# The v projection's causal convolution with tokens on the partitions: shifted rows by DMA in place of transposes, and a later opening of the late tiles

## The chip, the cores and the metric

The kernel runs on one core of one Trainium2 chip. The metric is device time in microseconds (us) of one execution. Before the change the median of three runs is 1875.9 us (1875.82 to 1875.97).

## The reference

One decoder layer over 256 tokens of width 2048, all in float32. Cut to what bears on the change:

```python
xn = rms_norm(h, ln_mix_g)                      # (256, 2048)
proj = einsum('btd,de->bte', xn, w_in)          # q, k, v, z, b, a, sc_b, sc_c, sc_h, gate_a, gate_b
qkv = silu(causal_dwconv(concat([q, k, v]), conv_w))   # 4 taps along the tokens, per channel
#   causal_dwconv: y[t] = sum_i x[t - 3 + i] * w[i]
q, k = l2_norm(q), l2_norm(k)                   # per head of 128 channels
o_a = gated_delta_chunked(q, k, v, g, beta)     # 16 heads; then rms_norm(o) * silu(z)
o_b = sc_b * causal_dwconv(sc_c * sc_h, conv_sc_w)
merged = sigmoid(gate_a) * (o_a @ w_proj_a) + sigmoid(gate_b) * (o_b @ w_proj_b)
h = h + merged @ w_out
ff = silu(hn @ w_gate) * (hn @ w_up);  out = rms_norm(h + ff @ w_down)
```

## The kernel before

**Tiling.** The 256 tokens are two halves (m = 0, 1) of 128. Every projection is cut into pieces of 512 output columns, called products: `product` (from L392) multiplies all 16 (for the last matrix 44) blocks of 128 input rows with one such piece. A matrix product is done three times, high part by high part, low by high and high by low, because float32 operands are split into two parts that TensorE takes. The weights come in groups of two blocks: `raw` (128 rows by 1024 numbers, 512 KB, by DMA from L263 in `fetch`), then `wh` by ScalarE (ACT), the rounded high part, then `wl` by VectorE (DVE), the rest. `ensure` issues them four groups ahead of TensorE. There are four `raw` buffers and four each of `wh` and `wl`. `raw36` is the load of group 36; a product with 16 blocks takes eight groups, so groups 0 to 7 are the first k product, 8 to 15 the first q product, and so on.

**Two forms of a product.** With `chan=True` the channels lie on the partitions of the result: 24 matmuls of 256 columns a group, 192 a product. With `chan=False` the tokens do: 12 matmuls of 512 columns a group, 96 a product.

**The order of the products.** For each of four groups g of four heads: k, z of the group before (from g = 1 on), q, v. Then for n = 0 to 3 the three short convolution products scc, sch and scb (with z of the last group after the first scc). Then gates, projections, w_out, and the feed-forward part.

**What sets the order of the rest.** All instructions are issued by hand in an order that a Python planner writes: `Pace` holds estimated times of each engine, every piece of work beside the products is a generator (`post_qk`, `post_v`, `core`, `post_b`, ...) that yields a due time, and `step` puts its next instructions between the matmuls when the planner thinks that they are due. Each engine runs its instructions in the order written, and so does SP's DMA queue: a DMA that has to wait holds up all DMAs behind it. The tickets in `turn` let the generators pass one after the other.

**v before.** In `post_v` (L800) the first v product (g = 0) has its channels on the partitions and is evacuated by DVE; the other three have tokens there, are evacuated by ACT (`rows_v`) and turned by DVE in 16 pieces (`flip`, `fc_v`). The convolution then runs along the free axis with four ACT and twelve DVE instructions (`conv`, `cv_v`), ACT applies silu, TensorE turns the result back with eight transposes a group (`vt`), and ACT scales and evacuates it in eight pieces to `v`. `core` uses `v` in `solve`.

**The late tiles.** `post_b` (L1164) ends an scb product. For n = 1 it first waits until the last head group is finished (`oc`), since `open_late` frees that group's memory and opens new tiles there; only then does it evacuate its PSUM tile. `product` allows one product with an unevacuated result when the next begins.

Of the kernel before, what the change touches and what calls it, by code (L numbers as in the profile page):

```python
# [9 lines left out]
F32 = mybir.dt.float32  # L10
F32R = mybir.dt.float32r
I32 = mybir.dt.int32
AF = mybir.ActivationFunctionType
ALU = mybir.AluOpType

P = 128
T = 256
D = 2048
KD = D // P
H = 16  # L20
HG = 4
NG = H // HG
DFF = 5632
KF = DFF // P
W = 512
# [7 lines left out]
MM = 4  # L33
LOWLAG = 1
EARLY = 16
LAG = 500.0
LOAD = 271
SOON = -1
# [161 lines left out]
def tile_gdn_shortconv_layer(  # L200
# [13 lines left out]
    ln_ffn: bass.AP,  # L214
    ln_fin: bass.AP,
    cqkv: bass.AP,
    csc: bass.AP,
    a_log: bass.AP,
    dt_bias: bass.AP,
# [4 lines left out]
    pace = Pace()  # L224
    pe = Lane(pace, nc.tensor, "pe")
    act = Lane(pace, nc.scalar, "act")
    dve = Lane(pace, nc.vector, "dve")
    pool = Lane(pace, nc.gpsimd, "pool")
    PS = bass.MemoryType.PSUM
    NS = D // W  # L230
# [15 lines left out]
    apool = pool_of("apool", 1)  # L246
    const = pool_of("const", 1, top=True)
    rawpool = pool_of("rawpool", 2, top=True)
    io = pool_of("io", 2, top=True)
# [6 lines left out]
    gp = pool_of("gp", 1, stack=pg)  # L256

    def bank(nm):
        return ps_sm.tile([P, 512], F32, tag="sm", name=nm)

    def fetch(dst, src, free=0.0):

        nc.sync.dma_start(dst, src)  # L263
        start = max(pace.t["dma"], free)
        pace.t["dma"] = start + 4.0 * math.prod(dst.shape) / 360.0
        pace.note(dst, "dma", True, pace.t["dma"] + Pace.DMA_LAG)

    def both(out, a, b, op):

        dve.scalar_tensor_tensor(out=out, in0=a, scalar=1.0, in1=b, op0=ALU.mult, op1=op)  # L270
# [4 lines left out]
    def pair(pool, tag, nm):  # L275
        t = pool.tile([P, 2, HG, T], F32R, tag=tag, name=nm)
        return t[:, 0], t[:, 1]
# [96 lines left out]
    def need(key, n=0):  # L374
        while key not in st:
            yield n
        if at[key] + LAG > pace.t["pe"]:
            pace.end = max(pace.end, at[key])
            yield n
# [3 lines left out]
    turn = [0, 0]  # L383
# [64 lines left out]
    ident = gp.tile([P, P], F32, name="ident")  # L448
# [15 lines left out]
    sel = gp.tile([P, HG, SQ], F32R, name="sel")  # L464

    g_ffn = const.tile([P, KD], F32, name="g_ffn")
    wc = gp.tile([P, 3 * H, 4], F32, name="wc")
    wsc = const.tile([P, KD, 3], F32, name="wsc")
    alog = gp.tile([P, H], F32, name="alog")
    dtb = gp.tile([P, H], F32, name="dtb")  # L470
# [37 lines left out]
    rx_row = gp.tile([P, T], F32, name="rx_row")  # L508

    def evac_chan(pt, dst, b):  # L510

        if len(b.shape) == 2:
            b = b.unsqueeze(1).broadcast_to([P, HG, T])
        for m in range(2):
            cs = slice(2 * m, 2 * m + 2)
            dve.tensor_tensor(
                dst[:, cs], pt[m].rearrange("p (c t) -> p c t", t=T), b[:, cs], op=ALU.mult
            )
        close(pt)

    def bc(ap, n):
        return ap.unsqueeze(2).broadcast_to([P, ap.shape[1], n])

    def rows_tile(nm):
        return io.tile([P, 2, W], F32, tag="rows", name=nm)

    def full_tile(nm):
        return io.tile([P, HG, T], F32, tag="rows", name=nm)

    def chan_tile(nm):  # L530
        return io.tile([P, HG, T], F32, tag="cv", name=nm)
# [3 lines left out]
    def evac_rows(pt, dst, func=AF.Copy):  # L535
        for m in range(2):
            act.activation(dst[:, m, :], pt[m], func, scale=rx[:, m:m + 1])
        close(pt)

    def flip(rows, ch, when=SOON):  # L540
        src = rows.rearrange("p m (c n) -> p m c n", n=P)
        dst = ch.rearrange("p c (m t) -> p m c t", t=P)
        for i in range(0, P, SQ):
            for j in range(0, P, SQ):
                dve.transpose(
                    out=dst[j:j + SQ, :, :, i:i + SQ], in_=src[i:i + SQ, :, :, j:j + SQ]
                )
            yield when

    def conv(chan, wt, taps, y, when, then=None):  # L550
        for c in range(HG):
            act.activation(y[:, c, :], chan[:, c, :], AF.Copy, scale=wt(c, taps - 1))
        yield
        for c in (0, 2):
            for s in range(1, taps):
                for j in (c, c + 1):
                    dve.scalar_tensor_tensor(
                        out=y[:, j, s:], in0=chan[:, j, :T - s], scalar=wt(j, taps - 1 - s),
                        in1=y[:, j, s:], op0=ALU.mult, op1=ALU.add,
                    )  # L560
            yield when
            if then is not None:
                act.activation(then[:, c:c + 2], y[:, c:c + 2, :], AF.Silu)

    xg = [pair(apool, f"a{n}", f"xg{n}") for n in range(NS)]
    oa = [pair(apool, f"s{n}", f"oa{n}") for n in range(NS)]

# [228 lines left out]
        mark(("sc", g), (s_, vs, rq))  # L798

    def post_v(g, pt, me):  # L800
        while turn[0] < me - 1:
            yield
        nm = f"v{g}"
        if g == 0:
            yield from need("rx_row")
            full = full_tile(f"full_{nm}")
            evac_chan(pt, full, rx_row)
            yield
        else:
            rows = rows_tile(f"rows_{nm}")  # L810
            evac_rows(pt, rows)
            yield
            while turn[0] < me:
                yield
            full = io.tile([P, HG, T], F32, tag="fc", name=f"fc_{nm}", bufs=1)
            yield from flip(rows, full)
        while turn[0] < me:
            yield
        y = chan_tile(f"cv_{nm}")
        yield from conv(full, lambda c, i: wc[:, 2 * H + HG * g + c, i:i + 1], 4, y, 0, y)  # L820
        turn[0] += 1
        yield
        yield from need(("sc", g))
        if g:
            yield from need(("done", g - 1))
        yield 2
        vs = st["sc", g][1]
        v = gp.tile([P, 2, HG, P], F32, tag="v", name=f"v_{g}")
        for m in range(2):
            b = bank(f"vt_{g}_{m}")  # L830
            for c in range(HG):
                pe.transpose(
                    b[:, c * P:(c + 1) * P], y[:, c, m * P:(m + 1) * P], ident
                )
            for c in range(HG):
                act.activation(
                    v[:, m, c, :], b[:, c * P:(c + 1) * P], AF.Copy, scale=vs[:, m, c:c + 1]
                )
        mark(("v", g), v)

    def post_z(g, pt):
# [47 lines left out]
    def core(g):  # L889
# [6 lines left out]
        s_, vs, rq = st["sc", g]  # L896
# [3 lines left out]
        for cp in range(2):  # L900
            pairs = []
            for c in (2 * cp, 2 * cp + 1):
                b = bank(f"gr0_{g}_{c}")
# [14 lines left out]
            b = bank(f"gr1_{g}_{cp}")  # L918
            bv = b.rearrange("p (c q n) -> p c q n", c=2, q=2)
            for j in range(2):  # L920
                c = 2 * cp + j
# [5 lines left out]
            for j in range(2):  # L927
                c = 2 * cp + j
# [36 lines left out]
        for j in range(SQ - 1):  # L965
            n = j // RS + 1
# [83 lines left out]
        v = st["v", g]  # L1050
# [47 lines left out]
        ro, _ = rsqrt(ssq.rearrange("p m c -> p (m c)"), 2 * HG, f"o{g}", 1.0 / P)  # L1098
# [5 lines left out]
        for hp in range(2):  # L1104
            b = bank(f"oc_{g}_{hp}")
            bv = b.rearrange("p (h t) -> p h t", t=T)
            for j in range(2):
                for m in range(2):
                    pe.transpose(bv[:, j, m * P:(m + 1) * P], ov[:, m, 2 * hp + j, :], ident)
            views.append(bv)  # L1110
        for hp, bv in enumerate(views):
            sl = slice(2 * hp, 2 * hp + 2)
            split(oa[g][0][:, sl, :], oa[g][1][:, sl, :], bv)
# [7 lines left out]
    for g in range(NG):  # L1121
        pt = product(xg, KD, f"k{g}", after=None if g else after_first, chan=True)
        if g == 0:
            scalars()
            spawn(spread())
            spawn(scalars2())
        spawn(post_qk(g, 0, pt, ticket()))
        spawn(decay(g))
        last = spawn(core(g))
        if g:  # L1130
            product_z(g - 1)
        pt = product(xg, KD, f"q{g}", chan=True)
        spawn(post_qk(g, 1, pt, ticket()))
        pt = product(xg, KD, f"v{g}", chan=g == 0)
        spawn(post_v(g, pt, ticket()))


# [26 lines left out]
    def post_b(n, pt, me):  # L1164
        while turn[0] < me - 1:
            yield
        if n == 1:
            yield from need(("oc", NG - 1))
            open_late()
        rows = rows_tile(f"scb{n}")  # L1170
        evac_rows(pt, rows)
        yield
        while turn[0] < me:
            yield
        y = st["y", n]
        ch = io.tile([P, HG, T], F32, tag="fc", name=f"bf{n}", bufs=1)
        yield from flip(rows, ch)
        both(y, y, ch, ALU.mult)
        yield SOON
        if n == 0:  # L1180
            ob[0] = pair(apool, f"s{NS}", "ob0")
        split(*ob[n], y)
        turn[0] += 1
# [3 lines left out]
    def open_late():  # L1187
        pg.close()
        lp = late["pool"] = pool_of("late", 1)
        ob[1:] = [pair(lp, f"s{NS + i}", f"ob{i}") for i in (1, 2, 3)]  # L1190
        late["xh"] = lp.tile([P, 2, D], F32, name="xh")
# [256 lines left out]
```

## Time and profile before

| | before |
|---|---|
| median of 3 runs | 1875.9 us |
| profiled execution | 1876.75 us |
| its span (first to last instruction) | 1875.0 us |
| TensorE (PE) busy | 1861.5 us, 99% |
| VectorE (DVE) busy | 1288.7 us, 69% |
| ScalarE (ACT) busy | 920.7 us, 49% |
| GpSimd (POOL) busy | 198.7 us, 11% |
| DMA engines busy, SP's queue | 54.8% of 16 engines |
| moved | 359.21 MB, 192 GB/s in the mean |
| granted TensorE clock, mean | 0.998 of full |

A busy TensorE only says that matmuls overlap without a gap. Whether it is held up is read from the chain that ended last (which engine the time was on) and from the list of waits (who waited for whom, how long in all).

### The profile page before, as it was taken

How to read it: one execution, taken by the hardware profiler on the slowest of the kernel's cores; microseconds unless marked ns; L12 is line 12 of the kernel's file. 1: busy time of each engine (PE TensorE's matmuls, PEld its weight loads, DVE VectorE, ACT ScalarE, POOL GpSimd, SP SyncE). 2: the span in 40 equal slices, each digit the busy share in tenths (PEclk: the TensorE clock that was granted, in tenths of full speed). 3: DMA queues.
4: the chain of work that ended last, by engine and by line, in shares of the span. 5: the costliest groups of instructions: out<-in, count | busy, mean ns of one | idle time of the engine just before them, and what ended most of it. 6: DMA issues, size and time to landing. Idle time of an engine off the chain costs nothing.

```text
span 1875.0 us, 25127 instructions
## 1 busy us (share of the span) xinstructions
PE 1861.5 (99%) x9444; PEld 1579.2 (84%) x9444; DVE 1288.7 (69%) x1826; ACT 920.7 (49%) x1186; POOL 198.7 (11%) x352
## 2 busy tenths in 40 slices
PE   9999999999999999999999999999999999999998
PEld 9999899988888888888888888888888888888886
DVE  6878788688885977454577789666666666645454
ACT  6755665676545445444444455444444444433443
POOL 0018145172170000000000000000000000000000
PEclk9999999999999999999999999999999999999999
DMA  8546545365464556665555565555555555665553
GB/s 305 189 161 203 186 161 198 133 200 196 144 207 140 195 194 213 208 210 195 186 190 192 188 205 188 204 193 195 195 191 192 194 187 191 202 219 195 193 192 134
DMA packets 101546, 359.21 MB, mean 192 GB/s; under 512 B 12320, under 2 KB 12576, under 8 KB 101168
## 3 DMA queue, kind: packets, MB, share of 16 engines
q1 hardware_dynamic: 98432, 349.69, 54.8%
q0 software_dynamic: 2848, 7.90, 1.5%
q8 instruction: 74, 1.21, 0.3%
q14 instruction: 48, 0.39, 0.1%
q10 hardware_dynamic: 144, 0.01, 0.0%
HBM read 354.38 MB, written 3.18 MB: 191 GB/s over the span
## 4 chain that ended last, share of the span: by engine, by line
PE 96%; DVE 2%; ACT 1%; DMA 1%; issue 1%; DVEq 0%; ACTq 0%
PE mm_dn L173 13%; PE mm_fu L173 13%; PE mm_fg L173 13%; PE mm_proj L173 9%; PE mm_gate L173 9%; PE mm_v L173 5%; PE mm_sch L173 5%; PE mm_scb L173 5%; PE mm_out L173 5%; PE mm_scc L173 4%; PE mm_q L173 4%; PE mm_k L173 4%; PE mm_z L173 4%; PE gr L173 1%; DMA raw<-in_w_in_dram 1%
## 5 line engine op out<-in xcount | busy, mean ns | idle before, releaser
L194 DVE SCALAR_TENSOR_TENSOR wl<-raw,wh 128x1024 fp32r<-128x1024 f32 (+1 forms) x652 | 791.4, 1223 | 481.8 <-ACT wh L194 475.8
L194 ACT CAST wh<-raw 128x1024 fp32r<-128x1024 f32 (+1 forms) x652 | 679.8, 1044 | 880.6 <-PE mm_fu L173 132.4
L173 PE MATMUL mm_dn<-wh,ff 128*128 128x512 f32 x704 | 216.8, 389 | 0.0
L173 PE MATMUL mm_fg<-wh,hg 128*128 128x512 f32 x704 | 216.7, 389 | 0.0
L173 PE MATMUL mm_fu<-wh,hg 128*128 128x512 f32 x704 | 216.7, 389 | 0.0
L173 PE MATMUL mm_gate<-wh,xg 128*128 128x512 f32 x512 | 157.5, 389 | 0.0
L173 PEld LDWEIGHTS mm_dn<-wh,ff 128*128 128x128 f32 x704 | 132.1, 188 | 27.6
L173 PEld LDWEIGHTS mm_fg<-wh,hg 128*128 128x128 f32 x704 | 132.1, 188 | 27.4
L173 PEld LDWEIGHTS mm_fu<-wh,hg 128*128 128x128 f32 x704 | 132.1, 188 | 27.4
L173 PE MATMUL mm_fg<-wl,hg 128*128 128x512 f32 x352 | 136.9, 389 | 0.0
L173 PE MATMUL mm_fu<-wl,hg 128*128 128x512 f32 x352 | 136.9, 389 | 0.0
L173 PE MATMUL mm_dn<-wl,ff 128*128 128x512 f32 x352 | 136.9, 389 | 0.0
L173 PEld LDWEIGHTS mm_gate<-wh,xg 128*128 128x128 f32 x512 | 96.1, 188 | 19.9
L173 PE MATMUL mm_gate<-wl,xg 128*128 128x512 f32 x256 | 99.6, 389 | 0.0
L173 PE MATMUL mm_q<-xg,wh 128*128 128x256 f32 x512 | 93.8, 285 | 0.0
L173 PE MATMUL mm_k<-xg,wh 128*128 128x256 f32 x512 | 93.0, 284 | 0.1
L173 PE MATMUL mm_sch<-wh,xg 128*128 128x512 f32 x256 | 79.9, 393 | 1.5 <-ACT scc L194 1.5
L173 PEld LDWEIGHTS mm_k<-xg,wh 128*128 128x128 f32 x512 | 80.3, 193 | 0.6 <-ACT wh L194 0.5
L173 PEld LDWEIGHTS mm_q<-xg,wh 128*128 128x128 f32 x512 | 79.9, 191 | 0.5
L173 PE MATMUL mm_z<-wh,xg 128*128 128x512 f32 x256 | 80.2, 395 | 0.0
L173 PE MATMUL mm_scc<-wh,xg 128*128 128x512 f32 x256 | 79.8, 393 | 0.0
L173 PE MATMUL mm_scb<-wh,xg 128*128 128x512 f32 x256 | 79.1, 390 | 0.0
(261 smaller groups left out, 2973.1 us busy)
## 6 DMA issues: line engine op xcount, KB each, us to landing
raw<-in_w_in_dram SPq DMA_DIRECT2D x284, 512.0 KB, 4.2
raw<-in_w_gate_dram SPq DMA_DIRECT2D x88, 512.0 KB, 4.1
raw<-in_w_up_dram SPq DMA_DIRECT2D x88, 512.0 KB, 4.0
raw<-in_w_down_dram SPq DMA_DIRECT2D x88, 512.0 KB, 4.3
raw<-in_w_pb_dram SPq DMA_DIRECT2D x32, 512.0 KB, 4.3
raw<-in_w_pa_dram SPq DMA_DIRECT2D x32, 512.0 KB, 4.4
raw<-in_w_out_dram SPq DMA_DIRECT2D x32, 512.0 KB, 4.3
raw<-in_w_in_dram SPq DMA_DIRECT2D x8, 256.0 KB, 5.9
```

Source lines behind the costliest of these rows:

```text
L173: return f(*a, **k)
L194: return f(*a, **k)
```

## The change

v keeps its tokens on the partitions in all four groups. The rows that the causal convolution needs from 1, 2 and 3 tokens earlier are made by DMA: for each shift s one copy of 128 - s partitions of `rows_v` to partitions s and up of a tile `sh`, and one of the last s rows of the first half to the first s rows of the second. The four taps' weights are loaded broadcast over all partitions (`wv`, 128 x 2048). Seven DVE instructions of 128 x 1024 multiply and add, ACT applies silu once, and two DVE instructions scale by `vs` into `v`. No transposes are left in `post_v`. The tile `oa` of the last head group is taken later, since its place holds `wv`. In `post_b` the wait and `open_late` stand after the evacuation, the turning and the product, ahead of the split.

```diff
+FAR = 2500.0
-    oa = [pair(apool, f"s{n}", f"oa{n}") for n in range(NS)]
+    oa = [pair(apool, f"s{n}", f"oa{n}") for n in range(NS - 1)]
...
     def post_v(g, pt, me):
         while turn[0] < me - 1:
             yield
-        nm = f"v{g}"
-        if g == 0:
-            yield from need("rx_row")
-            full = full_tile(f"full_{nm}")
-            evac_chan(pt, full, rx_row)
-            yield
-        else:
-            rows = rows_tile(f"rows_{nm}")
-            evac_rows(pt, rows)
-            yield
-            while turn[0] < me:
-                yield
-            full = io.tile([P, HG, T], F32, tag="fc", name=f"fc_{nm}", bufs=1)
-            yield from flip(rows, full)
+        rows = rows_tile(f"rows_v{g}")
+        evac_rows(pt, rows)
+        wv = apool.tile([P, 4, W], F32, tag=f"s{NS - 1}", name=f"wv_{g}")
+        fetch(wv.rearrange("p i n -> p (i n)"), cv_rows[g].partition_broadcast(P))
+        yield
         while turn[0] < me:
             yield
-        y = chan_tile(f"cv_{nm}")
-        yield from conv(full, lambda c, i: wc[:, 2 * H + HG * g + c, i:i + 1], 4, y, 0, y)
+        shifted = {}
+        for s, tag, k in ((1, "fc", {"bufs": 1}), (2, "rows", {}), (3, "cv", {})):
+            t = shifted[s] = io.tile([P, 2, W], F32, tag=tag, name=f"sh{s}_{g}", **k)
+            dve.memset(t[:s, 0, :], 0.0)
+            fetch(t[s:], rows[:P - s], pace.t["pe"])
+            fetch(t[:s, 1, :], rows[P - s:, 0, :])
+        pace.end = max(pace.end, pace.t["dma"] + FAR)
+        y = io.tile([P, 2, W], F32, tag="cv", name=f"y_v{g}")
+        def tap(s, dst, src):
+            both(dst, src, wv[:, 3 - s, :].unsqueeze(1).broadcast_to([P, 2, W]), ALU.mult)
+        tap(0, y, rows)
+        yield
+        for s, t in shifted.items():
+            tap(s, t, t)
+            both(y, y, t, ALU.add)
+            yield
+        act.activation(y, y, AF.Silu)
         turn[0] += 1
...
         for m in range(2):
-            b = bank(f"vt_{g}_{m}")
-            for c in range(HG):
-                pe.transpose(b[:, c * P:(c + 1) * P], y[:, c, m * P:(m + 1) * P], ident)
-            for c in range(HG):
-                act.activation(v[:, m, c, :], b[:, c * P:(c + 1) * P], AF.Copy, scale=vs[:, m, c:c + 1])
+            both(v[:, m], y[:, m].rearrange("p (c n) -> p c n", n=P), bc(vs[:, m], P), ALU.mult)
...
-        pt = product(xg, KD, f"v{g}", chan=g == 0)
+        pt = product(xg, KD, f"v{g}", chan=False)
...
     def post_b(n, pt, me):
-        if n == 1:
-            yield from need(("oc", NG - 1))
-            open_late()
         rows = rows_tile(f"scb{n}")
...
         both(y, y, ch, ALU.mult)
         yield SOON
+        if n == 1:
+            yield from need(("oc", NG - 1))
+            open_late()
```

SP's queue around group 36, the fifth group of the first z product, before the change (a `raw` is a weight load of 128 rows by 1024 numbers):

```order
L263 DMA raw34_1369<-in_w_in_dram 128x1024
L263 DMA raw35_1400<-in_w_in_dram 128x1024
L263 DMA raw36_1441<-in_w_in_dram 128x1024
L263 DMA raw37_1489<-in_w_in_dram 128x1024
L263 DMA raw38_1507<-in_w_in_dram 128x1024
```

And with the change (`sh1_0`, `sh2_0` and `sh3_0` are the rows of the first v product shifted by 1, 2 and 3 tokens):

```order
L265 DMA raw35_1305<-in_w_in_dram 128x1024
L265 DMA sh1_0_1324<-rows_v0_1052 127x1024
L265 DMA sh1_0_1324<-rows_v0_1052 1x16x32
L265 DMA sh2_0_1328<-rows_v0_1052 126x1024
L265 DMA sh2_0_1328<-rows_v0_1052 2x512
L265 DMA sh3_0_1332<-rows_v0_1052 125x1024
L265 DMA sh3_0_1332<-rows_v0_1052 3x512
L265 DMA raw36_1355<-in_w_in_dram 128x1024
L265 DMA raw37_1397<-in_w_in_dram 128x1024
```

Six DMAs stand between two weight loads. In the other three head groups the same six stand behind `raw60`, `raw95` and `raw130`; a seventh (`wv`) stands earlier, behind `raw27`, `raw59`, `raw91` and `raw123`. The one row of `sh1_0`'s second DMA is issued as 16 pieces of 32 numbers, the 127, 126 and 125 rows are issued as they are.

TensorE inside the first z product before the change (`mm_z` are its two PSUM tiles, `vt` the transposes of v):

```order
L173 MATMUL mm_z_1425<-wh_1490,xg_135 128x512 x2
L173 MATMUL mm_z_1425<-wl_1491,xg_135 128x512
L173 MATMUL vt_0_1615<-ident,cv_v_1419 128x128 x4
L173 MATMUL vt_1_1624<-ident,cv_v_1419 128x128 x4
L173 MATMUL mm_z_1424<-wh_1508,xg_136 128x512 x2
L173 MATMUL mm_z_1424<-wl_1509,xg_136 128x512
```

The same matmuls (blocks of the group that reads `xg_135`, then of the next) with the change:

```order
L174 MATMUL mm_z_1339<-wl_1399,xg_135 128x512
L174 MATMUL mm_z_1338<-wh_1398,xg_135 128x512 x2
L174 MATMUL mm_z_1338<-wl_1399,xg_135 128x512
L174 MATMUL mm_z_1339<-wh_1398,xg_135 128x512 x2
L174 MATMUL mm_z_1339<-wl_1399,xg_135 128x512
L174 MATMUL mm_z_1338<-wh_1416,xg_136 128x512 x2
```

No row with `vt` is left on TensorE, here or in the other three groups; nothing takes its place.

ACT near the end of the last head group before the change (`scc2` and `scb1` are evacuations of two products, `oa3` the result of the head group):

```order
L194 CAST wh186_6523<-raw186_6522 128x1024
L194 CAST wh187_6561<-raw187_6560 128x1024
L194 ACTIVATE scc2_6566<-mm0_scc2_6280,rx_132 128x512
L194 ACTIVATE scc2_6566<-mm1_scc2_6281,rx_132 128x512
L194 CAST oa3_140<-oc_3_0_6577 128x512
L194 CAST oa3_140<-oc_3_1_6582 128x512
L194 CAST wh188_6598<-raw188_6597 128x1024
L194 ACTIVATE scb1_6617<-mm0_scb1_6093,rx_132 128x512
L194 ACTIVATE scb1_6617<-mm1_scb1_6094,rx_132 128x512
```

And with the change, where the evacuation of `scb1` stands eight weight groups earlier:

```order
L195 COPY R_3_5483<-rc_3_5896 32x4x32 x8
L195 CAST wh179_6079<-raw179_6078 128x1024
L195 ACTIVATE scb1_6098<-mm0_scb1_5897,rx_132 128x512
L195 ACTIVATE scb1_6098<-mm1_scb1_5898,rx_132 128x512
L195 CAST wh180_6108<-raw180_6107 128x1024
```

It moved ahead of the head group's last steps; `scc2` keeps its place behind them.

## Rows read from the trace of the kernel before

**Rows 1.** The page: busy time, share of the span, instructions of each engine.
```profile
PE 1861.5 (99%) x9444; PEld 1579.2 (84%) x9444; DVE 1288.7 (69%) x1826; ACT 920.7 (49%) x1186; POOL 198.7 (11%) x352
```

**Rows 2.** The page: the chain that ended last, by engine.
```profile
PE 96%; DVE 2%; ACT 1%; DMA 1%; issue 1%; DVEq 0%; ACTq 0%
```

**Rows 3.** TensorE's waits: engine, line, waited for: us in total, times, longest.
```profile
PE mm_sch L173 <- ACT scc L194: 1.5, 1, 1.5
...
PE z L173 <- DVE mt L194: 0.8, 1, 0.8
```

**Rows 4.** Pieces of that chain in order of time: start us, us, what.
```profile
57.48 1.44 PE mm_v L173 x12
...
60.52 21.79 PE mm_v L173 x180
...
83.22 23.02 PE mm_k L173 x192
106.24 0.92 PE ssb_q L173 x8
...
127.75 0.87 PE vt L173 x8
...
158.03 21.79 PE mm_v L173 x96
...
420.88 21.80 PE mm_z L173 x96
```

**Rows 5.** Timeline 586 to 612 us: start, us, engine, instruction [idle before, releaser].
```profile
601.71 1.26 ACT L194 ACTIVATE scc<-mm_scc,rx 128x512 f32<-128x512 f32 x2
...
602.45 0.73 PE L173 MATMUL mm_sch<-wh,xg 128*128 128x512 f32 x2 [1.50 <-ACT scc L194]
...
607.13 1.26 ACT L194 ACTIVATE scb<-mm_scb,rx 128x512 f32<-128x512 f32 x2
```

**Rows 6.** DMA: queues (packets, MB, share); issues (count, KB, us to landing).
```profile
q1 hardware_dynamic: 98432, 349.69, 54.8%
...
q10 hardware_dynamic: 144, 0.01, 0.0%
...
raw<-in_w_in_dram SPq DMA_DIRECT2D x284, 512.0 KB, 4.2
...
out_dram<-xh SPq DMA_DIRECT2D x8, 256.0 KB, 2.4
...
g_mix<-in_ln_mix_dram ACTq DMA_DIRECT2D x1, 8.0 KB, 3.8
```

**Rows 7.** Two early stretches: busy time by engine, granted PEclk, DMA share, GB/s.
```profile
core 0: us, PE busy (x) PEld busy (x) DVE busy (x) ACT busy (x) POOL busy (x), PEclk, DMA share, GB/s
...
2.00:4.00 2.00, 2.00 (x11) 2.00 (x10) 0.00 (x0) 0.74 (x2) 1.51 (x4) 1.00 0.80 257
...
16.00:20.00 4.00, 4.00 (x36) 4.00 (x35) 2.82 (x3) 2.44 (x3) 0.00 (x0) 1.00 1.06 422
```

**Rows 8.** The page: the weight splits (count, busy us, mean ns, idle before).
```profile
L194 DVE SCALAR_TENSOR_TENSOR wl<-raw,wh 128x1024 fp32r<-128x1024 f32 (+1 forms) x652 | 791.4, 1223 | 481.8 <-ACT wh L194 475.8
L194 ACT CAST wh<-raw 128x1024 fp32r<-128x1024 f32 (+1 forms) x652 | 679.8, 1044 | 880.6 <-PE mm_fu L173 132.4
```

**Rows 9.** Timeline of TensorE from 0 us: the transposes at the start.
```profile
1.44 4.53 PE L460 MATMUL warm<-ident 128*128 128x128 f32 x20 [1.44 <-POOL ident masks.py:199]
```

**Rows 10.** DVE's groups, shapes apart: v's pieces, a 128 x 1024 product.
```profile
L194 DVE STREAM_TRANSPOSE fc_v<-rows_v 32x256 f32<-32x256 f32 x48 | 20.9, 436 | 0.8
...
L194 DVE SCALAR_TENSOR_TENSOR cv_v<-fc_v,wc,cv_v 128x254 f32<-128x254 f32 x12 | 5.2, 478 | 0.0
...
L194 DVE SCALAR_TENSOR_TENSOR sy<-sy,bf 128x1024 f32<-128x1024 f32 x4 | 4.9, 1237 | 0.0
```

More of the change, by code (lines that the diff above doesn't have):

```diff
@@ L216, in tile_gdn_shortconv_layer @@
     cqkv: bass.AP,
+    cv_rows: bass.AP,
     csc: bass.AP,
@@ L466, in tile_gdn_shortconv_layer @@
     g_ffn = const.tile([P, KD], F32, name="g_ffn")
-    wc = gp.tile([P, 3 * H, 4], F32, name="wc")
+    wc = gp.tile([P, 2 * H, 4], F32, name="wc")
     wsc = const.tile([P, KD, 3], F32, name="wsc")
@@ L825, in post_v @@
             yield from need(("done", g - 1))
-        yield 2
         vs = st["sc", g][1]
@@ L829, in post_v @@
         for m in range(2):
-            b = bank(f"vt_{g}_{m}")
-            for c in range(HG):
-                pe.transpose(
-                    b[:, c * P:(c + 1) * P], y[:, c, m * P:(m + 1) * P], ident
-                )
-            for c in range(HG):
-                act.activation(
-                    v[:, m, c, :], b[:, c * P:(c + 1) * P], AF.Copy, scale=vs[:, m, c:c + 1]
-                )
+            both(v[:, m], y[:, m].rearrange("p (c n) -> p c n", n=P), bc(vs[:, m], P), ALU.mult)
         mark(("v", g), v)
@@ L1110, in core @@
             views.append(bv)
+        if g == NG - 1:
+            oa.append(pair(apool, f"s{g}", f"oa{g}"))
         for hp, bv in enumerate(views):
@@ L1428 @@
         ("ln_fin", np.ascontiguousarray(np.broadcast_to(a["ln_final_g"], (P, D)))),
-        ("cqkv", np.ascontiguousarray(a["conv_qkv_w"][0].reshape(4, 3 * H, P).transpose(2, 1, 0))),
+        ("cqkv", np.ascontiguousarray(a["conv_qkv_w"][0][:, :2 * D].reshape(4, 2 * H, P).transpose(2, 1, 0))),
+        (
+            "cv_rows",
+            np.ascontiguousarray(
+                a["conv_qkv_w"][0][:, 2 * D:].reshape(4, NG, W).transpose(1, 0, 2).reshape(NG, 4 * W)
+            ),
+        ),
         ("csc", np.ascontiguousarray(a["conv_sc_w"][0].reshape(3, KD, P).transpose(2, 1, 0))),
```

## The prediction

> **What bounds the kernel now.** I read the busy shares first: TensorE is busy for 1861.5 of 1875.0 us, and DVE, the next, for 69% [rows 1]. Then the chain that ended last, which lies on TensorE for 96% [rows 2], and TensorE's waits: the two longest inside the kernel are 1.5 us in front of one sch product and 0.8 us in front of a step of the head groups [rows 3]. So TensorE's stream is the time. A matmul taken out of it pays in full; work moved between DVE and ACT pays nothing as long as it stays off TensorE's path. For the same reason TensorE has no idle time that could absorb a late weight group: what hides a late load is only the lead of the weight loads. The profiled execution took 1876.75 us, 1.75 us of it outside the span, and is 0.85 us above the median of the runs; I sum against 1876.75 and take 0.85 off at the end.
>
> **What is removed.**
> - Transposes of v: eight a group, 0.87 us in a piece of the chain [rows 4], four groups: -3.5 us.
> - The first v product changes its form. As 192 matmuls of 256 columns it takes 1.44 + 21.79 = 23.2 us, its neighbour k 23.0; in the form with 96 matmuls a v product takes 21.8 [rows 4]: -1.3 us.
> - The later opening: sch had waited 1.50 us for the evacuation of scc2 [rows 5], since scb1's tile, free only with the evacuation at 607.13, could not be its place. In ACT's new order scb1 is evacuated eight weight groups earlier, so sch finds a free tile: -1.5 us. At worst the wait stays (0).
>
> Together -6.3 us.
>
> **DVE and ACT.** From g = 1 on DVE loses 16 turning pieces of 0.436 and 12 convolution steps of 0.478 us [rows 10], 12.7 us, and gains seven products of 128 x 1024, near 1.24 us each [rows 10], two scalings of half that size, 1.2, and three memsets that the trace does not show; bounded by nothing and by a whole 128 x 1024 product each, 0 to 3.7 us. That is 9.9 to 13.6 us, about as much as before. In g = 0 there was nothing to turn, so it is some 5 us more. I cost it at nothing: `wl` is made ahead of need, and DVE is idle for 481.8 us in front of `wl` [rows 8]; without that cover each microsecond would be TensorE's. ACT only loses work.
>
> **The DMAs that are added.** Per group six shift DMAs with 378 rows of 4 KB, plus a few short ones, and one broadcast load. The order puts the shifts into SP's queue between two weight loads: behind raw35, raw60, raw95 and raw130. They cannot start before the squared sums of q are through TensorE (`ssb_q`, whose operand's place sh1 takes), in g = 1 also not before the evacuation of v. Every later weight load stands behind them. So the question is how soon the engines are through with them, and the trace of before shows no copy from SBUF to SBUF and no DMA whose rows are not a multiple of 32.
>
> Two bounds. If 127 rows are spread like 128, eight for each of 16 engines, the three copies take 24 rows an engine. With all engines busy they move 422 GB/s at a share of 1.06 [rows 7], 26.4 GB/s each, 0.155 us a row: 3.7 us. If rows are dealt out only in equal shares, 127 is prime and goes to one engine, 126 goes to 14 engines in nines, 125 to five in twenty-fives; if each begins at the same engine, that one gets 127 + 9 + 25 = 161 rows, 25.0 us (0.193 us a row by the mean of SP's queue, 349.69 MB in 54.8% of 16 engines of 1875 us [rows 6], gives 31).
>
> I take the second, and it is a choice. The row nearest to it is the one queue with a single load, g_mix: 144 packets for 128 rows of 64 bytes [rows 6], so 16 packets more than rows, as if each of 16 equal shares had one closing packet. And in the new order the single row of 2 KB is issued as 16 pieces, while 127 x 1024 is left in 127 rows: what could be cut into 16 equal parts was cut, the 127 was not. Against it: it is not shown that the engines need equal shares.
>
> The Trainium skill ("DMA: Bandwidth & Descriptors", section "Why a DMA increments its semaphore by 16 and not by 1") states that a DMA issued from SP uses the largest number of engines, up to 16, that divides its slowest dimension, from the lowest-numbered engine up, and that 127 partitions go to one. By that rule the sum is the one below; without it the gain of 6.3 us would stand nearly alone. The 144 packets agree with it, but no run here has 127 rows yet.
>
> **What the shifts cost then.** A weight load has eight rows on the crowded engine too, behind the 161. From the first shift's issue to a usable group: about 2 us of fixed latency (256 KB land in 2.4 us, 512 KB in 4.2 [rows 6], less 0.6 and 1.2 of transfer: 1.8 to 3.0), 169 rows of 0.155 = 26.2, `wh` 1.04 and `wl` 1.22 [rows 8]: 30.5 us. TensorE has this much to do meanwhile, with 2.72 us a group in the token form (21.80 / 8) and 2.88 in the channel form (23.02 / 8) [rows 4]:
> - g = 0: four groups of z (32 to 35), 10.9 us; late by 19.6.
> - g = 1: five groups of k (56 to 60), 14.4, and `ssb_q` 0.9; the queue starts 1.3 us later, with v's evacuation (2 x 0.65); late by 16.5.
> - g = 2: half a k product (92 to 95), 11.5; late by 19.0.
> - g = 3: one group of scc and three of z (127 to 130), 10.9; late by 19.6.
>
> Sum 74.7 us. Behind the late load the next ones follow at about 1.2 us against a need of 2.7, so one stall a group is all; DVE has finished its other work by then, and the taps, placed two or three `wl` later, find their rows landed.
>
> After such a pause TensorE may restart slowly. At the kernel's start 20 transposes took 4.53 us [rows 9], while eight of the same size take 0.87 in the middle [rows 4], so 20 would take 2.2; half the pace, that of the 1.2 GHz level, though the granted clock of 2 to 4 us already reads 1.00 [rows 7]. I take 2 us for each of four restarts, 8 us, with 0 and 12 as bounds.
>
> Sum: 1876.75 - 6.3 + 74.7 + 8 = 1953.2, in the runs **1952 us**. Its own range: 1929 if only the 127 rows crowd one engine and the others spread (-11), restarts cost nothing (-8) and the latency is 1 us less each (-4); 1990 with 0.193 us a row (+26), slow restarts (+4) and 2 us more of latency each (+8).
>
> **Rivals.**
> - *The rows spread over all engines.* For it: nothing in the trace forbids it, and every DMA there ran at full rate. The chain of 30.5 us becomes 2 + 24 rows of 0.155 + short pieces 0.5 + the load's own 1.2 + 2.3 = 9.7 us, under every cover (10.9 the smallest). TensorE never waits and the gain stands: 1870.5, in the runs 1870 us. It decides at some 30 rows on one engine for the three copies: above that the tightest groups stall. Against it: the 16 closing packets and the uncut 127.
> - *Spread, but slower than loads from HBM.* Copies from SBUF to SBUF might run at half the rate or issue slowly, with DVE's memsets and 5 more microseconds in g = 0 near the limit. Each group is then late by 1 to 3 us: -6.3 + 4 to 12, 1874 to 1881, I say 1876. For it: covers are only about 1 us longer than need. Against it: the loads' 4.2 us include the same steps.
> - *The change does not take the transposes away.* It does: no such row is left in the order; this has no chance of its own.
>
> **Chances and range.** Crowded engine 0.82, spread 0.13, spread but late 0.05. By the crowded case the time is 1952; with the rivals at 0.18 the range must hold nearly all of that case, so I widen its own range to 1890 to 2005 for partial crowding and for followers that I have not priced. What a measurement of this kernel can tell from no change is about 0.2%, 3.75 us. Faster by more than that: 0.13 (the spread case). Within it: 0.03. Slower: 0.84.
>
> **What the new profile would show.** Right: four waits of TensorE of 15 to 20 us for `wh` or `wl`, in the first z, the third k, the third z and the last z product; the DMA sh1 landing more than 20 us after its issue, and raw36, raw61, raw96 and raw131 far above 4.2 us; four slices with low GB/s; 96 matmuls of 21.8 us for the first v, no `vt`, no wait of sch for scc. Wrong: sh1 landing after 4 to 8 us and TensorE's waits as short as before (rival one), or several waits of 1 to 3 us (rival two). If sh1 takes 20 us and TensorE still does not wait, the lead of the loads is longer than I counted.

## The result, and the profile after

The changed kernel takes 1984.6 us, median of 4 runs (1983.5 to 1986.3), against 1875.9 before: ratio 1.0581, 95% interval 1.0568 to 1.0594. It is 108.7 us slower; 76 were forecast.

The page after, with busy time, TensorE's busy tenths and granted clock in 40 slices of 49.6 us, GB/s, SP's queue and the chain:

```profile
PE 1867.8 (94%) x9316; PEld 1577.4 (79%) x9316; DVE 1291.0 (65%) x1776; ACT 902.1 (45%) x1134; POOL 197.6 (10%) x352
...
PE   9959499499599999999999999999999999999997
...
PEclk9979799799799999999999999999999999999999
...
GB/s 296 216 103 189 148 160 192 120 162 195 117 165 197 184 158 201 198 209 205 204 191 181 198 193 202 193 195 194 183 192 203 196 193 193 193 218 192 192 194 134
...
q1 hardware_dynamic: 100768, 360.10, 52.8%
...
PE 90%; DMA 4%; SPq 3%; DVE 1%; ACT 1%; issue 1%; DVEq 0%; ACTq 0%
```

TensorE does 128 matmuls fewer than in [rows 1], is about as busy, and idles in four slices (5, 4, 4 and 5 tenths), in which the memory traffic dips and the clock reads 7. DMA and SP's queue now hold 7% of a chain of which TensorE held 96% [rows 2]. The four holes are three rows of TensorE's waits:

```profile
PE mm_z L174 <- ACT wh L195: 50.7, 2, 26.6
...
PE mm_k L174 <- ACT wh L195: 26.8, 2, 26.0
...
PE mm_z L174 <- DVE wl L195: 24.7, 1, 24.7
```

102.2 us, from 115, 221, 367 and 512 us on: first z, third k, third z and last z product. The two short waits of [rows 3] are gone. The chain of the changed kernel from 106 us on shows how the first hole comes about (start, us, what):

```profile
105.42 0.93 PE ssb_q L174 x8
...
106.36 0.78 SPq L265
...
107.19 8.01 SPq L265
...
115.25 1.17 SPq L265
...
118.59 18.52 DMA sh<-rows_v
...
137.24 0.10 DVE full_k L195
```

As soon as `ssb_q` is through, SP issues the shifts, and the last of them lands at 137.1. In the timeline of the same stretch the instructions that came late carry what they waited for:

```profile
106.36 16.27 SPq L265 DMA_DIRECT2D sh<-rows_v  x6
122.68 8.78 SPq L265 DMA_DIRECT2D raw<-in_w_in_dram  x3
...
137.24 1.29 DVE L195 TENSOR_TENSOR full_k<-mm_k,rx_row 128x512 f32<-128x512 f32 x2 [27.09 <-DMA sh<-rows_v]
138.45 1.22 DVE L195 SCALAR_TENSOR_TENSOR wl<-raw,wh 128x1024 fp32r<-128x1024 f32 x1
...
138.38 1.04 ACT L195 CAST wh<-raw 128x1024 fp32r<-128x1024 f32 x1 [31.99 <-DMA raw<-in_w_in_dram]
...
139.72 0.79 PE L174 MATMUL mm_z<-wl,xg 128*128 128x512 f32 x1 [24.73 <-DVE wl L195]
```

Two things are late together. ACT waits for the weight load behind the copies, as forecast. DVE waits too: `full_k`, the evacuation of the next k product, takes the place of `rows_v`, which the copies still read, and the `wl` of a group that had long been loaded is queued behind it. In the other three groups the weight load alone decides: here the third k and, with its SP rows, the third z:

```profile
207.32 0.66 SPq L265 DMA_DIRECT2D sh<-rows_v  x1
...
245.44 1.04 ACT L195 CAST wh<-raw 128x1024 fp32r<-128x1024 f32 x1 [35.42 <-DMA raw<-in_w_in_dram]
...
355.55 18.07 SPq L265 DMA_DIRECT2D sh<-rows_v  x6
373.67 9.93 SPq L265 DMA_DIRECT2D raw<-in_w_in_dram  x4
...
392.56 1.04 ACT L195 CAST wh<-raw 128x1024 fp32r<-128x1024 f32 x1 [36.98 <-DMA raw<-in_w_in_dram]
```

What the DMA engines do meanwhile, 109 to 115 us (packets, MB, share of 16 engines):

```profile
DMA packets 34, 0.14 MB, mean 23 GB/s; under 512 B 0, under 2 KB 0, under 8 KB 34
...
q1 hardware_dynamic: 34, 0.14, 6.0%
```

6.0% of 16 engines is about one engine (6.25%): the 127 rows go through it alone, one in 0.176 us (6 us / 34), while the loads of before ran at 422 GB/s [rows 7]. This is the equal dealing that the prediction chose; the Trainium skill ("DMA: Bandwidth & Descriptors", section "Why a DMA increments its semaphore by 16 and not by 1") says it of 127 partitions, and the trace agrees.

TensorE behind the first hole (stretch, us, busy with count, granted clock, DMA share, GB/s):

```profile
139.70:144.20 4.50, 4.48 (x11) 0.50 0.36 120
144.20:148.70 4.50, 4.50 (x23) 1.00 0.70 226
...
393.60:396.00 2.40, 2.31 (x5) 0.50 0.11 39
396.00:400.00 4.00, 4.00 (x11) 0.50 0.79 247
```

The last two rows stand behind the third hole. After 25 us without a matmul TensorE runs at 0.50, the 1.2 GHz level, for 4.5 us, and does 11 matmuls of 512 columns. At 0.227 us each (21.80 / 96 [rows 4]) it would have done 20; of the 23 in the next row some are shorter. Behind the other holes the clock reads 0.50 for longer or about as long: 7.0, 6.6 and 4.4 us. Half of these 22.5 us, about 11, is lost.

### The profile page after: what moved, and what is told of

Same layout as the page of the kernel before. It is cut to its first block, busy times and chain, and to the rows that moved or that the text cites. A ratio compares the mean times of both kernels' runs of the same rounds, so it can differ in the third digit from the quotient of the medians.

```text
span 1984.6 us, 24805 instructions
## 1 busy us (share of the span) xinstructions
PE 1867.8 (94%) x9316; PEld 1577.4 (79%) x9316; DVE 1291.0 (65%) x1776; ACT 902.1 (45%) x1134; POOL 197.6 (10%) x352
## 4 chain that ended last, share of the span: by engine, by line
PE 90%; DMA 4%; SPq 3%; DVE 1%; ACT 1%; issue 1%; DVEq 0%; ACTq 0%
PE mm_dn L174 12%; PE mm_fu L174 12%; PE mm_fg L174 12%; PE mm_gate L174 9%; PE mm_proj L174 9%; PE mm_v L174 4%; PE mm_out L174 4%; PE mm_sch L174 4%; PE mm_q L174 4%; PE mm_z L174 4%; PE mm_scc L174 4%; PE mm_scb L174 4%; SPq L265 3%; PE mm_k L174 3%; DMA raw<-in_w_in_dram 3%; DMA sh<-rows_v 1%
## 5 line engine op out<-in xcount | busy, mean ns | idle before, releaser
L174 PE MATMUL mm_z<-wh,xg 128*128 128x512 f32 x256 | 85.1, 415 | 50.7 <-ACT wh L195 50.7
L174 PEld LDWEIGHTS mm_z<-wh,xg 128*128 128x128 f32 x256 | 50.4, 201 | 61.8 <-ACT wh L195 51.3
```

Source lines behind the costliest of these rows:

```text
L174: return f(*a, **k)
```

## The experiments

Times are medians; ratios are to the kernel before on the same chip, with 95% intervals. Of each edit only the lines that matter are shown. Where copies are moved, joined or left out, the planner goes on reckoning with them as before, in lines not shown, so that the other instructions keep their order (but for the run with another FAR).

**The copies cut into equal shares** (in `fetch`; CUT is 112, LENS (127, 126, 125)).

```
+        n = dst.shape[0]
+        cut = CUT if CUT < n < P and n in LENS else 0
+        if cut:
+            nc.sync.dma_start(dst[:cut], src[:cut])
-        nc.sync.dma_start(dst, src)
+        nc.sync.dma_start(dst[cut:], src[cut:])
```

> The changed kernel with each of its three long shift copies cut in two: 127 rows as 112 + 15, 126 as 112 + 14, 125 as 112 + 13. Nothing else moves on any engine, only SP's queue has 12 more entries. Theory (crowded engine): a copy's rows are dealt to the DMA engines in equal shares only, so 127 rows all went to one engine and the weight load queued behind them waited for that engine. Cut, an engine has 7 + 1 rows of each copy, 24 in all, some 4 us; the weight load behind lands 8 to 10 us after the first shift is issued, TensorE has 8 to 13 us of work left at that point in the four groups, so the four waits of 24 to 27 us shrink to at most 2 us each, and the time is 1868 to 1876 us. Rival (copies inside SBUF are slow, or SP's sequencer is slow to issue them): same bytes and twice as many entries in the queue, so the four waits stay at 20 us or more and the time is 1975 to 1995 us.

1888.0 us, ratio 1.0068 (1.0054 to 1.0082). 96.6 of the 108.7 us are gone with nothing else moved, and with twelve entries more in SP's queue. So the rival falls: that part of the loss was the dealing of rows. But 1868 to 1876 was missed by 12 us. The longest waits that are left, and SP in that stretch:

```profile
PE mm_z L176 <- DVE wl L197: 3.6, 3, 2.5
PE mm_z L176 <- ACT wh L197: 2.7, 2, 1.8
```

```profile
105.90 0.65 SPq L270 DMA_DIRECT2D sh<-rows_v  x1
...
111.18 1.57 SPq L271 DMA_DIRECT2D sh<-rows_v  x2
112.79 1.36 SPq L271 DMA_DIRECT2D raw<-in_w_in_dram  x3
```

SP waits until 105.9 and then needs 6.9 us to issue nine DMAs; the weight load goes out at 112.8.

**Only the 127 rows cut** (the same edit with LENS (127,)).

> The changed kernel with only the 127-row copy cut (112 + 15); 126 and 125 rows stay whole. Theory (crowded engine): the first engine has 7 + 1 + 9 + 25 rows and 8 of the weight load behind them, 50 rows instead of 169, at 0.165 to 0.19 us a row 8.3 to 9.5 us, with 4.3 us around them 12.6 to 13.8 from the first issue to a usable weight group; TensorE has 8.2, 13.0, 11.2 and 10.5 us of work left there (read from the changed kernel's trace), so it waits 4 to 6, 0 to 1, 1 to 3 and 2 to 3 us, 8 to 13 in all: 1876 to 1886 us. Rival (each copy slow by itself, whatever its row count): a third of the loss goes, 1945 to 1955 us.

1902.6 us, 1.0140 (1.0126 to 1.0154): nearer to the crowded engine (1876 to 1886) than to equal prices (1945 to 1955), yet outside both. Three quarters of the loss hang on the 127 rows. Its first `wh` comes 14.5 us after the first shift's issue (106.14 to 120.66) where 10.3 to 11.5 were summed, and the slow restarts were left out of the expectation.

**Three aligned copies of 128 rows** in place of nine DMAs.

```
-            dve.memset(t[:s, 0, :], 0.0)
-            fetch(t[s:], rows[:P - s], pace.t["pe"])
-            fetch(t[:s, 1, :], rows[P - s:, 0, :])
+            nc.sync.dma_start(t, rows)
...
```

> The changed kernel with each shift replaced by one aligned copy of all 128 rows (so nothing is shifted and v is not the convolution), three DMAs a group on SP in place of nine in the cut version; the three small memsets are left out. Rows per engine are the same 24. Theory A (in the cut version the rest of the loss is the time in which SP issues nine DMAs, 6.9 us in front of the weight load): issue takes about 2 us, the weight load is 5 us earlier, no wait above 0.5 us is left: 1870 to 1876 us. Theory B (the rest is the passage of 24 rows an engine, and the wait of SP for the place of the first copy): 1883 to 1890 us as in the cut version.

1879.1 us, 1.0021 (1.0012 to 1.0031), 9 below the cut version. It lies between the theories, 3 above A's upper end and 4 below B's lower one. SP's rows there:

```profile
105.83 1.99 SPq L817 DMA_DIRECT2D sh<-rows_v  x3
107.87 2.95 SPq L265 DMA_DIRECT2D raw<-in_w_in_dram  x3
```

The load goes out 4.9 us earlier, as A has it, with the same rows on each engine and the same wait of SP in front of the first copy. So most of what the cut version still lost goes with the issue of nine DMAs. A's "no wait above 0.5 us" failed: 1.1 us for a `wl` and 3.1 in all (longest 1.9) of z for `mt` are left. The latter is not the copies' doing: the version without any copy, below, has 5.0 us of it and takes 1879.7.

**The long copies on POOL's queue, then all six.**

```
-            fetch(t[s:], rows[:P - s], pace.t["pe"])
+            nc.gpsimd.dma_start(t[s:], rows[:P - s])
```

> The changed kernel with the three long shift copies (127, 126 and 125 rows, uncut) issued from POOL's queue instead of SP's; the short ones stay on SP. Theory (crowded engine, and the loss comes from standing in front of the weight loads in SP's queue): the weight loads no longer stand behind the copies, so the four waits go to 0 to 5 us each whether the rows crowd one engine or not: 1869 to 1890 us. If POOL's queue deals rows the same way, a shift still takes 20 us to land and the taps on DVE start late; if it spreads them over all engines, it lands within 8 us. Rival (copies inside SBUF slow the engines for everyone, whatever queue they stand in): the weight loads stay late, waits of over 10 us in each group, above 1920 us.

1906.4 us, 1.0165 (1.0151 to 1.0179): between both. The uncut copies land in 5 to 8 us (issues from 107 to 109 us), with all engines at work (queues from 109 to 114 us):

```profile
sh<-rows_v POOLq DMA_DIRECT2D x1, 508.0 KB, 5.0
...
q0 software_dynamic: 335, 1.21, 98.5%
```

So POOL's queue deals 127 rows over all engines. The Trainium skill ("DMA: Bandwidth & Descriptors", section "Why a DMA increments its semaphore by 16 and not by 1") names this as an exception for some copies from that queue, and the trace agrees. I took the rest for SP's wait in front of the short copies.

> The changed kernel with all six shift copies, uncut, issued from POOL's queue, so that SP's queue has nothing but weight loads and the broadcast there. Theory: with only the long ones on POOL, SP still stood 10 us in front of the first short copy and issued the weight load at 109.4 us in place of 99.9; now it is issued at 99 to 100 us as in the kernel before, is through before the copies start, and TensorE waits less than 1 us in each of the four groups: 1870 to 1876 us. Rival (the copies' rows on the 16 engines are what delays the weight loads, since rows of POOL's queue were served before theirs): waits of 3 to 9 us a group as with the long ones alone on POOL, 1895 to 1906 us.

1905.4 us, 1.0158 (1.0143 to 1.0173): this theory fell. The time lies in the rival's 1895 to 1906, but not for the rival's reason: the weight load went out at 99.0 us and landed in 4.1, and TensorE was late all the same. DVE's waits:

```profile
DVE sh L195 <- DMA sh<-rows_v: 26.1, 3, 9.9
...
DVE full_k L195 <- DMA sh<-rows_v: 5.8, 2, 5.1
```

I concluded that the taps stood too early in DVE's order.

**All on POOL, taps later** (`FAR = 10000.0` in place of 2500).

> The version with all six shift copies on POOL's queue, with the taps put later in DVE's order (FAR 10000 in place of 2500; the planner then also moves some work of the head groups). Theory (new, from the trace of that version: the weight loads were on time there, landed 4 us after their issue, but DVE stood 26 us in front of the first taps of groups 1 to 3 and 5 us in front of full_k of the next k, which takes the place of the rows that the copies still read; the split of the next weight group is queued behind): DVE's waits in front of the taps go, the one in front of full_k in group 0 stays, TensorE's waits of 5.5, 5.7 and 10 us go with their slow restarts, 1905 becomes 1877 to 1884 us. Rival (the rows of the copies on the 16 engines themselves hold up TensorE's weights): stays at 1895 to 1906 us.

1907.4 us, 1.0165 (1.0151 to 1.0179): that theory fell too, and the time is 1 above the rival's range. DVE waits 6 us for taps, no longer 26, but 11.8 in front of a `full_k`. The timeline in front of the 10 us hole:

```profile
449.00 0.22 POOL L195 TENSOR_TENSOR rb<-rb,tb 128x8 f32<-128x8 f32 x1
449.54 0.59 POOL L817 DMA_DIRECT2D sh<-rows_v  x1 [0.31 <-issue]
...
459.23 1.26 ACT L195 ACTIVATE scc<-mm_scc,rx 128x512 f32<-128x512 f32 x2 [17.78 <-DMA d<-rb]
```

POOL issues the copies only when its triangular solve (`rb`, `tb`) of the head group is done, at 449.5. ACT's evacuation of scc takes the place of `rows_v` and waits until they are through: the last, issued at 452.18, lands 7.0 us later, at 459.2. (The row names `d<-rb`, the DMA behind them on POOL's queue; with only the long copies there, the same wait of 15.2 us names `sh<-rows_v`.) Everything behind it on ACT is late, weight splits included; the run before this one has the same wait of scc, 17.6 us, in front of its longest hole (9.8 us), which its DVE rows do not show. So on POOL the copies come late; they are not slow there.

**The cut copies on ACT's queue** (`nc.scalar.dma_start` for all nine).

> The cut version (112 + 15, 112 + 14, 112 + 13 rows) with its nine shift DMAs issued from ACT's queue instead of SP's. Theory: SP's weight loads no longer stand behind the copies, which land 3 to 5 us after issue as in the aligned version; but ACT is in their issue for 9 x 0.7 = 6.5 us, and the next wh is queued behind: in groups 1 to 3 TensorE waits 0 to 2 us each, in group 0 about 2.5 as before (full_k): 1876 to 1884 us, less than the 1888 of the cut version on SP. Rival (the issue on ACT costs TensorE as much as on SP): 1886 to 1895 us.

1882.7 us, 1.0036 (1.0023 to 1.0050), inside the expectation. `full_k` still waits 5.5 us in group 0 and costs TensorE 3.1, and a new wait, z for `mt`, costs 2.8.

**No copies, with and without the products that used them.**

```
-            fetch(t[s:], rows[:P - s], pace.t["pe"])
-            fetch(t[:s, 1, :], rows[P - s:, 0, :])
...
-            tap(s, t, t)
+            tap(s, t, y)
```

The second version also leaves out `tap(s, t, ...)` and the addition behind it, six instructions a group.

> The changed kernel without its six shift copies per group: the taps read the running sum y instead of shifted rows (so v is not the convolution), the broadcast of the weights, the memsets and every DVE, ACT and TensorE instruction stay in their order. Theory: apart from the copies the change is what was summed, 3.5 us of transposes, 1.3 of the first v product and about 1 for the sch wait less, and DVE's new work costs nothing: 1869.5 to 1872 us. Rival (DVE's or ACT's moved work, or the 1 MB broadcast, also delays TensorE): 1874 to 1880 us, with waits for wl or wh of 1 us and more in the four groups.

1879.7 us (1876.6 to 1885.0), 1.0021 (1.0012 to 1.0031), above the expectation: without any copy the change loses. The time lies in the rival's range, but its waits for `wl` or `wh` are not there (0.2 us). TensorE waits elsewhere, where before it did not:

```profile
451.23 0.29 PE L174 MATMUL z<-mt,ua 128*32 128x32 f32 x2 [4.49 <-DVE mt L195]
```

> The version without shift copies, and without the six tap products per group on DVE that used them as well (the first product, y times the last weights, stays; v is not the convolution). Theory: what keeps the version without copies at 1879.7 us is that in its group 2 POOL's triangular solve took 49 us in place of 38 while DVE did long 128 x 1024 products, so that z came 4.7 us late; without the products the solve takes 37 to 40 us in all groups, no wait of z for mt above 0.5 us is left, and the time is 1869.5 to 1872 us. Rival (the lateness has nothing to do with DVE's products, but comes from the order or the broadcast load): 1876 to 1880 us, with z late again in group 2.

1871.7 us, 0.9978 (0.9969 to 0.9988): the theory, 8 us lower for six DVE products a group, and no wait for `mt` of 0.5 us or more. POOL's solve of group 2 (380 to 450 us), in the kernel before, without copies, and without copies and products:

```profile
L194 POOL TENSOR_TENSOR rb<-rb,tb 128x60 f32<-128x60 f32 (+24 forms) x31 | 17.9, 578 | 2.4
L194 POOL TENSOR_TENSOR tb<-rb,ub 128x60 f32<-128x60 f32 (+24 forms) x31 | 15.7, 507 | 6.3 <-DMA ub<-d 4.0
```

```profile
L195 POOL TENSOR_TENSOR rb<-rb,tb 128x60 f32<-128x60 f32 (+24 forms) x31 | 22.5, 726 | 2.4
L195 POOL TENSOR_TENSOR tb<-rb,ub 128x60 f32<-128x60 f32 (+24 forms) x31 | 22.0, 709 | 8.0 <-DMA ub<-d 5.6
```

```profile
L195 POOL TENSOR_TENSOR rb<-rb,tb 128x60 f32<-128x60 f32 (+24 forms) x31 | 20.9, 675 | 2.4
L195 POOL TENSOR_TENSOR tb<-rb,ub 128x60 f32<-128x60 f32 (+24 forms) x31 | 16.4, 530 | 6.1 <-DMA ub<-d 3.8
```

33.6, 44.5 and 37.3 us of work on the same 62 instructions. The trace without copies shows how, at 425 us:

```profile
424.97 1.31 DVE L195 SCALAR_TENSOR_TENSOR sh<-y_v,wv 128x1024 f32<-128x1024 f32 x1
425.28 1.13 POOL L195 TENSOR_TENSOR tb<-rb,ub 128x42 f32<-128x42 f32 x1
```

In the kernel before, the same step of the solve takes 0.27 us in this group. In all three traces every instruction of the solve over 0.9 us, 62 of 248 before, 84 without copies and 73 without copies and products, overlaps a DVE instruction of 128 x 1024 with two inputs (the weight split `wl` is one too); of the others, 0.2 to 0.4 us for the most part, hardly any starts inside one. So DVE's products slow POOL, and z, which hangs on the solve, comes late. Without products the solve was expected at 37 to 40 us in all groups; with the gaps between its instructions it was 42 to 46 in groups 0 to 2. In groups 0 and 1 it is as long with the products (45 and 44), which fall mostly outside it there; only in group 2 do the six lie inside (49 against 42).

> The version without shift copies once more, one look. Theory: POOL's solve is slowed by DVE's products by an amount that differs from run to run, but it is over 40 us in at least two of the groups 0 to 2 again, where the kernel before has 43, 37 and 38. Rival (the 49 us were one accident): 37 to 40 us in groups 1 and 2, and a time of 1872 us or less.

One run: 1876.7 us, the solve 47, 44 and 47 us long in groups 0 to 2 with its gaps (before 43, 37, 38), and TensorE's waits for `mt` only 1.2 us in all; 2.0 more are of y, the next step behind z, for `zt`. The slow solve recurs, and so does a time 5 us above the 1871.7; how much of the solve reaches TensorE differs between runs.

**The two parts that need no copy, alone.** First the later opening (`open_late` moved behind scb1's product, on the kernel before):

> The kernel before with only the later opening of the late tiles (behind scb1's product with y, in front of its split). Theory: TensorE's wait of 1.5 us in front of sch goes and nothing takes its place: 1874.4 us, 1.5 below the kernel before. Rival: another release becomes the last one and the wait stays: 1875.9 us.

1875.1 us, 0.9995 (0.9986 to 1.0004): not told from no change. The wait of [rows 5] is gone, and the largest group inside the kernel is now

```profile
PE oc L173 <- DVE zs L194: 0.7, 2, 0.5
```

Then with the first v product in the form of the others:

```
-        pt = product(xg, KD, f"v{g}", chan=g == 0)
+        pt = product(xg, KD, f"v{g}", chan=False)
...
```

> The kernel before with the two parts of the change that need no shift copy: the first v product in the form of the others (turned by DVE and convolved along the free dimension as for groups 1 to 3), and the later opening. Theory: 1.3 us of the product, less 8 transposes of 0.11 us for nothing else, and 0.8 us of the opening as measured alone: 1873.5 to 1874.5 us, 0.1% below the kernel before. Rival (16 more turning pieces on DVE in the first group make a step of the head groups late): 1875.5 to 1880 us.

1873.9 us, 0.9990 (0.9981 to 0.9999): 1.7 below the kernel before, as expected, and the fastest version here that leaves nothing out.

## Why the prediction was right, and where its sizes were off

The direction, the place and the cause held: four waits in the four products named, from rows that are dealt in equal shares, in front of the weight loads. The time (1984.6) lies inside the range and inside the crowded case's own 1929 to 1990, 32.6 us above the value taken. That it stays under 1990 is in part luck: room left for latency and a slower row took in causes that the prediction did not name.

- **Removed, -6.3.** No `vt` is left, the first v is 96 matmuls, sch waits no more: as forecast. Without copies and products, which is what this part is worth, it is 4.2 us (1871.7 against 1875.9), not 6.3: of the 1.5 from the opening 0.8 was measured, which is not told from nothing, since a wait of oc for `zs`, 0.7, came in its place. In the version without copies and products oc waits 1.1 and gr 0.8 for `ua`, new short waits of 1.9 us, about what is missing.
- **The stalls, 74.7: the mis-sized term.** They are 102.2. From the first issue to the weight load's landing I summed 2 + 26.2 = 28.2 us; from the first issue to the next `wh` it took 32.0, 38.1, 37.0 and 33.8 (third with its start at 355.55, fourth at 500.93 with `wh` at 534.77), 28 us more in all. One part is the row: 0.176 us, not 0.155, 3.5 us over 169 rows; with 2 + 169 x 0.176 = 31.7 the first group is explained. (The 0.155 took the loads' share of 1.06 for 1; with it the row is 0.165.) The 5 to 6 us more of the second and third group fall into stretches in which POOL's queue moves `em` and `gl`, 1 MB, through the same engines. The changed kernel's queues from 230 to 236 us (packets, MB, share of 16 engines):

```profile
q0 software_dynamic: 321, 1.13, 56.1%
q1 hardware_dynamic: 93, 0.30, 15.6%
```

 That this sharing is the cause was not tried by itself. Latency and rate had been allowed for in the range, the sharing had not.
- **The cover of group 0, 10.9.** It was 8.6: TensorE stopped at 115.0, 8.6 us after the first issue, one weight group early, since DVE's `full_k` held up a `wl`. The prediction named what stands behind SP's wait, but not who takes the place that the copies read from.
- **Restarts, 8.** About 11, inside the bounds of 0 and 12. With it the terms give -6.3 + 102.2 + 11 = 106.9 of the 109.6 us between the profiled executions (1986.34 and 1876.75); new short waits are most of the rest (oc for `zs` 1.1, k for `wl` 0.9, gr for `ua` 0.8).
- **DVE and ACT, nothing.** True in this kernel, where the six products that use the shifted rows start at 145 to 160, 249 to 258, 396 to 408 and 538 to 549 us, all outside POOL's solves (178 to 217, 328 to 367, 476 to 513 and 625 to 663). Without copies, and so without the holes, the same products cost 5 to 8 us (1876.7 and 1879.7 against 1871.7), at least in part by way of POOL. So the cover named, DVE's idle time in front of `wl` [rows 8], was not the only one to look at.
- **Rival one (1870).** The cut version is that case, and it took 1888. The rival's chain counted the short pieces as 0.5 us; the nine issues took 6.9, behind a wait of SP until 105.9 in which the kernel before had already issued the next load, at 99.9. With three issues it was 1879.1, no more than without any copy (1879.7), so the rest of the distance to 1870 is not the copies' but the products'.

## What to carry to other kernels

Before shifting a tile by DMA, look at the row counts: cut a copy whose count has no good divisor into a part with a multiple of 16 rows and a rest, and count the added issues too. Then ask for each queue what stands behind the copy, and for each place that it reads who wants to write there next, since a late copy stops those engines in order. Work that fits on an engine with idle time can still slow its neighbour: check the slack of the slowest chain, here POOL's solve, not only of the engine that gets the work.

## What the runs showed of the hardware that was not expected

- The queue that issues is held while one engine is crowded: six DMAs took 16.3 and 18.1 us to issue, two of them 8.8, against 6.9 for nine in the cut version and 2.0 for three aligned ones. It need not have set the end: 2 us and 169 rows one after the other (31.7 us) account for the 32.0 of the first group. Why the queue is held was not settled.
- Copies inside SBUF run below the rate of loads: in the cut version 107 to 113 us moved 1.42 MB, 237 GB/s, at 82% of the engines (18 GB/s a busy engine), where loads reach 422 GB/s at a share of 1.06 (25) [rows 7]. The stretch holds short packets too, 95 of 442 under 512 B, so how much is the copy's own is not shown.
- A POOL instruction of 0.2 to 0.4 us takes 1.1 to 1.4 in most cases beside a DVE one of 128 x 1024 with two inputs; 62 of them took 33.6 us before, 44.5 with the products among them and 37.3 without. The Trainium skill ("SBUF — State Buffer", section "Who interferes with whom") states that a DVE instruction with two SBUF inputs contends with a GpSimd one that reads SBUF, which is what both are here; the traces agree.
